# A hybrid decoder layer on one core: matmul order anew around the state scan, two scan products on four quarters, w_out's low parts by VectorE

## The chip, the core and the metric

The kernel runs on one core of one Trainium2 chip. The metric is the device time of one execution in microseconds (us). A figure is the median of several runs; the profile shows one execution.

## What is computed

One decoder layer for 512 positions of width 1024. The reference, cut to what matters here:

```python
h = rms_norm(x, pre_mix_norm)
proj = einsum('bsd,dc->bsc', h, w_in)        # q, k, v | qkv of the delta net | z | a | b
o_att = moba_attention(q, k, v, rel_bias)    # 8 heads of 64, blocks of 256 keys
o_gdn = gated_deltanet(qkv, z, a, b, ...)    # 8 heads of 64, chunks of 64
mix = einsum('bsc,cd->bsd', concatenate([o_att, o_gdn]), w_out)
x = x + rms_norm(mix, post_mix_norm)
h = rms_norm(x, pre_mlp_norm)
m = square(relu(h @ w_up)) @ w_down          # 1024 -> 4096 -> 1024
return x + rms_norm(m, post_mlp_norm)

# the scan in gated_deltanet, chunk by chunk
v_new = u_c - w_c @ state
o = q_c @ state + a_c @ v_new
state = state * gl + k_c^T @ v_new
```

## The kernel before, in words

All large products are made of three matmuls of rounded halves (high by high, low by high, high by low), so every weight chunk of 128x512 is loaded on SP's queue, cast to its high part on ACT (`wo_h`, `w_hi`) and subtracted to its low part (`wo_l`, `w_lo`). `load_split` (L116 to L123) does that for w_out; in the kernel before, its subtraction for w_out is on POOL. The raw chunks rotate through two buffers (`raws`, `w_raw`), so a load waits for the subtraction two chunks earlier.

The stages overlap. A main stream (`projections`) makes the 28 column blocks of h times w_in in the order of the string `ORDER`; it serves as filler. Beside it run `chunks` (normalisation, decay factors and the masked products of the delta net, four times), `inverse` (a triangular inverse by VectorE and small transfers), `scores` and `values` (attention), then `scan`, and after it `weights_out`, `output` and the MLP. PE's order is written out: the class `Weave` (L28 to L67) runs these streams as generators on an estimated PE clock `now`; a stream yields a delay from the table `WAIT` (or the name of a mark) and is resumed no earlier than that; of those that are ready the one of the lowest `RANK` goes first. So a number in `WAIT` moves matmuls on PE. On the other engines a scheduler orders the instructions, with `LEAD` as a priority for some streams. All engines work through their instructions in order.

In `scan` (L735 to L842) a tile t is 128 positions, two chunks c. For each tile: `U V` (tile names `vB,UT`, into the two banks `vo[0]`, `vo[1]`), for each chunk `S,LWQ` (state by the chunk's queries and keys), the copy of `vn` out of the bank (L818), `vn,kdec` (the update of the state), and at the tile's end `A' V` (`vn,AT`, into the other halves of the same banks), whose result ACT copies to `ot` (L839). U V and A' V have 16 products of 64x64 each, two matmul instructions to a product; a 64-row half of the array is chosen by c, a 64-column half by the rows of the bank that are written. `finish_o` (L847 on) normalises `ot` on DVE (L856) and transposes it on PE (`ident,ot`).

In attention, `scores` makes for a group p of two heads four products `pt` of 512, 384, 256 and 128 columns, DVE adds the bias and takes the minimum (L651, reading the bank `ps_a`), ACT takes the exponential (L653), PE transposes it (`ident,L`), ACT copies it (`ph`, L679) and PE multiplies it by V (`ph,V`). There are four groups, 0 to 3. `RC` (L508) is a DVE step of `chunks` whose result PE multiplies by `picks`.

`output` (L900 to L939) makes for each of four position tiles 48 matmuls `wo_h`, `wo_l` by `mg`, `ma`; a tile's two banks are chosen in `start`; `normed` (L940 on) normalises the result (L943, L948, L954) and PE transposes it (`ident,xs`). `up0` starts the MLP.

Of the kernel before, what the change touches and what calls it, by code (L numbers as in the profile page):

```python
# [16 lines left out]
DRAM = bass.MemoryType.DRAM  # L17
EPS = 1e-6

WAIT = {'h': 1.7, 'conv_k': 5.5, 'k': 3.6, 'conv_q': 6.15, 'q': 4.5, 'conv_v': 11.0, 'v': 6.02, 'z': 6.39, 'ab': 0.1, 'g': 11.93, 'scalars': 3.68, 'r_in': 0.8, 'r_out': 4.4, 'kk': 2.46, 'kk_out': 14.43, 'gl': 3.22, 'qk': 3.88, 'va': 1.1, 'a': 2.4, 'row': 1.38, 'rows': 4.0, 'pv': 1.54, 'att': 2.16, 'inverse': 0.9, 'merge': 10, 'p1': 1.5, 'p2': 1.7, 'w': 1.78, 'vn': 1.0, 'state': 1.12, 'o_in': 6.0, 'o': 3.3, 'wo': 0.88, 'wo_out': 17.6, 'normed': 6.44, 'n': 1.7, 'up': 1.9, 'sums': 1.5, 'turned': 0.5, 'pv0': 1.5}  # L20

RANK = {'chunks': 5, 'inverse': 3, 'scan': 3, 'scores': 4, 'values': 2, 'finish_o': 1, 'take': 4}
LEAD = {'chunks': 0, 'inverse': 100, 'scan': 100, 'scores': 0, 'values': 100, 'finish_o': 0, 'take': 0, 'take_a': 0}
START = (5.5, 9.0, 17, 16, 30, 10.5)
ORDER = "q0 k0 x0 k1 q1 q2 k2 k3 z0 q3 y0 x1 v0 w0 v1 y1 w1 v2 x2 v3 x3 y2 w2 y3 z1 w3 z2 z3"


class Weave:  # L28
# [38 lines left out]
def layer(ctx, tc, nc, x, w_in, w_ab, w_out, w_up, w_down, conv_w, a_log, dt_bias, gdn_norm_w, rel_bias,  # L67
# [96 lines left out]
    def kof(pair, k, cols=slice(0, 512)):  # L164
        return pair[k // 4][:, k % 4, cols]
# [259 lines left out]
    def scalars():  # L425

        w8 = lambda t: t[:, :128].rearrange("p (a b) -> p a b", a=8)
        abr = w8(tmp("abr"))
        abw = tmp("abw", FR)[:, :256].rearrange("p (k a b) -> p k a b", k=8, a=2)
        abh, abl = abw[:, :, 0], abw[:, :, 1]  # L430
        nc.sync.dma_start(abr, w_ab)
        yield "h2"
        split(abh, abl, abr)
        abT = bank(shape=(128, 4, 16))
        p_ab = bank()
        yield "h3"
        for k in range(8):
            mm(p_ab[:32], abw[:, k].rearrange("p a b -> p (a b)"), kof(hT_h, k), start=k == 0, stop=False, skip_group_check=True)
            mm(p_ab[:16], abh[:, k], kof(hT_l, k), start=False, stop=k == 7, skip_group_check=True)
        abs_ = tmp("abs")[:32]  # L440
        nc.scalar.copy(abs_, p_ab[:32])
        two = gpool.tile([32, 16], FT, name="two")
        tt(two, ident[:32, :16], ident[:32, 16:32], op=OP.add)
        yield WAIT["ab"]
        for t in range(4):
            mm(abT[:, t, :], abs_[:, 128 * t:128 * t + 128], two, start=True, stop=True)
        ab = gpool.tile([128, 4, 16], FT, name="ab")
        nc.scalar.copy(ab, abT)
# [286 lines left out]
    def scan():  # L735
# [62 lines left out]

        rows_c = [(slice(64 * c, 64 * c + 64), slice(64 - 64 * c, 128 - 64 * c)) for c in range(2)]
        head = lambda h: slice(64 * (h % 2), 64 * (h % 2) + 64)  # L800
        for t in range(4):
            o = sc.tile([128, 512], FT, name="ot", bufs=4)
            V = sc.tile([128, 512], FT, name="vn", bufs=1)
            vo = [bank(shape=(128, 4, 128)) for c in range(2)]
            for h in range(8):
                for c, (cs, _) in enumerate(rows_c):
                    mm(vo[c][cs, h // 2, head(h)], UT[cs, h, t], vB[cs, t, 64 * h:64 * h + 64], start=h == 0, stop=False, skip_group_check=True)
            weave.now -= 8 * 64 * 4 / 2400
            for c, (cs, oc) in enumerate(rows_c):
                n = 2 * t + c  # L810
                S, Sn = SS[n % 2], SS[(n + 1) % 2]
                if n:
                    for p in range(4):
                        wq = LWQ[p // 2][:, p % 2, t, c]
                        mm(vo[c][cs, p], wq[:, :64], S[:, p], start=False, stop=False, skip_group_check=True)
                        mm(vo[c][oc, p], wq[:, 64:], S[:, p], start=p == 0, stop=False, skip_group_check=True)
                    weave.now -= 4 * 128 * 4 / 2400
                nc.scalar.copy(V[cs], vo[c][cs].rearrange("p a b -> p (a b)"))  # L818
                yield WAIT["vn"]
                if n < 7:  # L820
                    sp = bank(shape=(128, 4, 64))
                    for h in range(8):
                        mm(sp[head(h), h // 2], kdec[cs, t, 64 * h:64 * h + 64], V[cs, 64 * h:64 * h + 64], start=True, stop=True)
                    weave.now -= 4 * 64 * 4 / 2400
                    for hh in range(2):
                        hs = head(hh)
                        if n:
                            tt(Sn[hs, :, hs], S[hs, :, hs], EGL[hs, :, n:n + 1].to_broadcast([64, 4, 64]), op=OP.mult)
                            tt(Sn[hs, :, hs], Sn[hs, :, hs], sp[hs], op=OP.add)
                        else:  # L830
                            nc.vector.tensor_copy(Sn[hs, :, hs], sp[hs])
                if c == 0:
                    yield WAIT["state"]
# [41 lines left out]
    def weights_out():  # L875
        yield "scan"
        for b in range(2):
            for z in (1, 0):
                if (b, z) == (1, 0):
                    mark("wo0", 2)  # L880
                    yield "projected"
                wh, wl = big("wo_h", dt=FR), big("wo_l", dt=FR)
                for k in range(4):
                    load_split(wh[:, k], wl[:, k], w_out[512 * z + 128 * k:512 * z + 128 * k + 128, 512 * b:512 * b + 512],
                               sub=nc.gpsimd.tensor_tensor)
                    W[b, 4 * z + k] = (wh[:, k], wl[:, k])
                    yield WAIT["wo"]
        mark("wo", WAIT["wo_out"])

    def output():  # L890
# [550 lines left out]
```

## Time and profile before

| | us |
|---|---|
| median of 3 runs | 662.05 (661.96 to 663.56) |
| profiled execution | 662.51 |
| its span in the trace | 660.7 |
| PE busy in the span | 632.4 |
| DVE busy | 437.6 |
| ACT busy | 360.5 |
| POOL busy | 200.0 |

The span runs from the first to the last instruction that the profiler saw; 1.8 us of the execution's time lie around it. Times in rows are counted from the span's start. Busy is the time in which an engine had an instruction at work; a matmul's listed duration holds its way through the array, so the distance between the starts of two rows says better what the first one took.

### The profile page before, as it was taken

What the parts mean: (1) busy time and instruction counts of PE and PEld (TensorE: products, weight loads), DVE (VectorE), ACT (ScalarE), POOL (GpSimd) and SP (SyncE); (2) the same over time, 40 slices, a digit from 0 to 9 for tenths busy, and PEclk for the clock granted to TensorE, in tenths of its full rate; (3) what the DMA queues carried; (4) which work ended last, traced back from release to release, by engine and by line L of the source; (5) the groups of instructions that cost most, each with busy time, mean ns of one, the idle gap of its engine ahead of it and who ended that gap; (6) DMA issues with size and microseconds to landing.
All of it is one profiled execution on the core that took longest, in us unless ns stands there. A gap on an engine that the chain in (4) does not pass through costs nothing.

```text
span 660.7 us, 11130 instructions
## 1 busy us (share of the span) xinstructions
PE 632.4 (96%) x4357; PEld 526.9 (80%) x4357; DVE 437.6 (66%) x627; ACT 360.5 (55%) x602; POOL 200.0 (30%) x231
## 2 busy tenths in 40 slices
PE   7899999899999999898999999999999999999995
PEld 4778777676687776676799899999998888887884
DVE  4358675997421335365445578878779888988775
ACT  5366564264636646854231675566566556665661
POOL 4355655332454236632302113111130130000002
PEclk9999999999999999999999999999999999999998
DMA  7232323223631202481249989899899999957503
GB/s 235 68 103 71 81 81 103 89 81 112 136 87 51 82 30 84 144 269 65 97 169 332 227 225 238 232 288 284 236 263 328 291 287 291 277 198 288 198 1 127
DMA packets 60226, 113.16 MB, mean 171 GB/s; under 512 B 15700, under 2 KB 34644, under 8 KB 59790
## 3 DMA queue, kind: packets, MB, share of 16 engines
q1 hardware_dynamic: 42446, 83.03, 36.4%
q0 software_dynamic: 17728, 29.43, 21.6%
q8 instruction: 34, 0.56, 0.3%
q14 instruction: 18, 0.15, 0.1%
HBM read 106.65 MB, written 35.15 MB: 215 GB/s over the span
## 4 chain that ended last, share of the span: by engine, by line
PE 80%; DVE 9%; ACT 5%; DMA 3%; POOL 1%; issue 1%; SPq 0%; DVEq 0%; POOLq 0%; ACTq 0%
PE ps_mm L77 41%; PE ps_g L77 21%; PE ps_a L77 14%; PE ps_a L81 2%; DVE conv L346 2%; PE ps_g L81 1%; DMA w_raw<-in_w_out 1%; DVE inv L726 1%; DVE pr L725 1%; DMA xx<-in_x 1%; DMA wd<-d_T 1%; DMA inv<-d_n 1%; ACT wo_h L122 1%; ACT ph L679 0%; DVE xs L948 0%
## 5 line engine op out<-in xcount | busy, mean ns | idle before, releaser
L135 POOL TENSOR_TENSOR w_lo<-w_raw,w_hi 128x512 fp32r<-128x512 f32 x54 | 70.7, 1311 | 116.1 <-ACT w_hi L134 115.8
L77 PE MATMUL ps_mm<-hT_h,w_hi 128*128 128x512 f32 (+1 forms) x224 | 93.1, 416 | 1.0 <-DVE conv L346 1.0
L77 PE MATMUL ps_mm<-hT_l,w_hi 128*128 128x512 f32 (+1 forms) x224 | 87.2, 389 | 0.0
L77 PE MATMUL ps_mm<-hT_h,w_lo 128*128 128x512 f32 (+1 forms) x224 | 86.7, 387 | 0.0
L110 ACT CAST wdh<-wd 128x1024 fp32r<-128x1024 f32 x53 | 55.9, 1054 | 52.0 <-PE ps_mm L77 23.5
L111 DVE TENSOR_TENSOR u_l<-w,u_h 128x1024 fp32r<-128x1024 f32 x46 | 56.2, 1224 | 37.8 <-ACT u_h L110 36.8
L111 DVE TENSOR_TENSOR wdl<-wd,wdh 128x1024 fp32r<-128x1024 f32 x53 | 64.9, 1225 | 22.8 <-ACT wdh L110 22.7
L110 ACT CAST u_h<-w 128x1024 fp32r<-128x1024 f32 x46 | 47.9, 1045 | 57.1 <-PE ps_a L77 19.7
L1123 POOL DMA_DIRECT2D d_T<-in_w_down x32 | 33.0, 1034 | 144.1 <-DMA d_T<-in_w_down 80.5
L134 ACT CAST w_hi<-w_raw 128x512 fp32r<-128x512 f32 x56 | 34.6, 620 | 46.0 <-PE ps_mm L77 26.2
L77 PEld LDWEIGHTS ps_mm<-hT_h,w_hi 128*128 128x128 f32 x224 | 42.8, 191 | 14.5 <-issue 6.3
L77 PEld LDWEIGHTS ps_mm<-hT_h,w_lo 128*128 128x128 f32 x224 | 43.0, 192 | 9.0
L77 PEld LDWEIGHTS ps_mm<-hT_l,w_hi 128*128 128x128 f32 x224 | 43.0, 192 | 6.4 <-DVE hT_l L111 0.2
L77 PE MATMUL ps_mm<-wdh,u_h 128*128 128x512 f32 x116 | 45.3, 390 | 0.0
L168 POOL TENSOR_SCALAR s<-s 128x1 f32<-128x1 f32 x12 | 3.8, 319 | 136.8 <-DVE s L1316 108.2
L77 PE MATMUL ps_mm<-wdl,u_h 128*128 128x512 f32 x116 | 45.1, 389 | 0.0
L77 PE MATMUL ps_mm<-wdh,u_l 128*128 128x512 f32 x116 | 45.1, 389 | 0.0
L346 DVE SCALAR_TENSOR_TENSOR conv<-ps_mm,cw,conv 128x511 f32<-128x511 f32 (+2 forms) x36 | 26.8, 745 | 18.0 <-ACT conv L343 17.5
L111 DVE TENSOR_TENSOR u_l<-f,u_h 128x1024 fp32r<-128x1024 f32 x28 | 34.1, 1219 | 0.0
L77 PE MATMUL ps_g<-wdh,u_h 128*128 128x512 f32 x80 | 31.2, 390 | 0.4 <-DVE y L1297 0.4
L651 DVE CUSTOM_DVE_ANT_0 L<-ps_a,E 128x512 f32<-128x512 f32 (+3 forms) x32 | 14.4, 487 | 25.7 <-PE ps_a L77 25.5
L77 PE MATMUL ps_g<-wdh,u_l 128*128 128x512 f32 x80 | 31.1, 389 | 0.0
(428 smaller groups left out, 1751.7 us busy)
## 6 DMA issues: line engine op xcount, KB each, us to landing
d_T<-in_w_down POOLq DMA_DIRECT2D x48, 512.0 KB, 10.6
wd<-d_T SPq DMA_DIRECT2D x32, 512.0 KB, 6.2
w<-in_w_up SPq DMA_DIRECT2D x28, 512.0 KB, 8.5
w_raw<-in_w_in SPq DMA_DIRECT2D x54, 256.0 KB, 2.6
wd<-in_w_down SPq DMA_DIRECT2D x24, 512.0 KB, 7.7
w_raw<-in_w_out SPq DMA_DIRECT2D x16, 256.0 KB, 2.7
d_T<-d_T POOLq DMA_DIRECT2D x8, 512.0 KB, 10.5
xx<-in_x SPq DMA_DIRECT2D x4, 512.0 KB, 6.6
```

What stands on the lines that cost most here:

```text
L77: nc.tensor.matmul(o, l, r, **kw)
L81: nc.tensor.transpose(o, i, ident[:k, :k])
L110: nc.scalar.copy(hi, src)
L111: tt(lo, src, f32(hi), op=OP.subtract)
L122: nc.scalar.copy(hi, raw)
L134: nc.scalar.copy(hi, raw)
L135: (sub or tt)(lo, raw, f32(hi), op=OP.subtract)
L346: stt(c[:, s:], p[:, :512 - s], cw[:, ft, j:j + 1], c[:, s:], op0=OP.mult, op1=OP.add)
L651: nc.vector.tensor_tensor_reduce(out=l, in0=s[hh][:, :w], in1=Es[hh][:, w - 1::-1], scale=1.0, scalar=3e38, op0=OP.add, op1=OP.min, accum_ ...
L725: tt(v, iN[:, 0:m, m:m + 1].to_broadcast([128, m, w]), iU[:, m:m + 1, m:32].to_broadcast([128, m, w]), op=OP.mult)
L726: tt(iU[:, 0:m, m:32], iU[:, 0:m, m:32], v, op=OP.subtract)
L1123: nc.gpsimd.dma_start(d_T[t][k], block(b, second)[k], accum_op=OP.add, max_dma_last_dim=1024)
```

## The change

- The tables. `WAIT`: k 3.6 to 2.95, z 6.39 to 7.99, r_in 0.8 to 0.72, gl 3.22 to 2.12, va 1.1 to 1.38, rows 4.0 to 3.2, att 2.16 to 1.3, o_in 6.0 to 3.6, o 3.3 to 3.73, normed 6.44 to 11.21. The others as in the diff.
- U V of the next tile and A' V of this tile are written in turn, so that consecutive matmuls go to four 64x64 quarters of the array. U V of both chunks is now in one bank `vb[t]`, A' V of both in one bank `ob[t]`.
- a, b: the matmuls of the low half take the 32 columns that those of the high half take (before 16).
- w_out's low parts are subtracted by VectorE.
- The output's position tiles take other banks.

```diff
-RANK = {'chunks': 5, 'inverse': 3, 'scan': 3, 'scores': 4, 'values': 2, 'finish_o': 1, 'take': 4}
-LEAD = {'chunks': 0, 'inverse': 100, 'scan': 100, 'scores': 0, 'values': 100, 'finish_o': 0, 'take': 0, 'take_a': 0}
-START = (5.5, 9.0, 17, 16, 30, 10.5)
-ORDER = "q0 k0 x0 k1 q1 q2 k2 k3 z0 q3 y0 x1 v0 w0 v1 y1 w1 v2 x2 v3 x3 y2 w2 y3 z1 w3 z2 z3"
+RANK = {'chunks': 5, 'inverse': 3, 'scan': 3, 'scores': 5, 'values': 5, 'finish_o': 1, 'take': 4}
+LEAD = {'chunks': 0, 'inverse': 0, 'scan': 100, 'scores': 0, 'values': 100, 'finish_o': 0, 'take': 0, 'take_a': 100}
+START = (5.5, 9.0, 17, 16, 30, 9.0)
+ORDER = "q0 k0 x0 k1 q1 q2 k2 k3 z0 q3 y0 x1 v0 w0 v1 y1 w1 v2 v3 x2 y2 w2 x3 y3 z1 w3 z2 z3"
...
-            mm(p_ab[:16], abh[:, k], kof(hT_l, k), start=False, stop=k == 7, skip_group_check=True)
+            mm(p_ab[:32], abw[:, k].rearrange("p a b -> p (a b)"), kof(hT_l, k), start=False, stop=k == 7, skip_group_check=True)
...
+        vb, ob = [bank(shape=(128, 4, 128))], []
+        def apart(t, V=None):
+            for h in range(8):
+                for c, (cs, oc) in enumerate(rows_c):
+                    if t < 4:
+                        mm(vb[t][cs, h // 2, head(h)], UT[cs, h, t], vB[cs, t, 64 * h:64 * h + 64], start=h == 0, stop=False, skip_group_check=True)
+                if V is not None:
+                    for c, (cs, oc) in enumerate(rows_c):
+                        mm(ob[t - 1][oc, h // 2, head(h)], AT[cs, h, t - 1], V[cs, 64 * h:64 * h + 64], start=t == 1 and not c and h == 0, stop=True, skip_group_check=True)
...
+        apart(0)
         for t in range(4):
...
-            vo = [bank(shape=(128, 4, 128)) for c in range(2)]
-            for h in range(8):
-                for c, (cs, _) in enumerate(rows_c):
-                    mm(vo[c][cs, h // 2, head(h)], UT[cs, h, t], vB[cs, t, 64 * h:64 * h + 64], start=h == 0, stop=False, skip_group_check=True)
+            ob.append(bank(shape=(128, 4, 128)))
...
-            for h in range(8):
-                for c, (cs, oc) in enumerate(rows_c):
-                    mm(vo[c][oc, h // 2, head(h)], AT[cs, h, t], V[cs, 64 * h:64 * h + 64], start=not t and not c and h == 0, stop=True, skip_group_check=True)
+            if t < 3:
+                vb.append(bank(shape=(128, 4, 128)))
+            apart(t + 1, V)
...
-                    load_split(wh[:, k], wl[:, k], w_out[512 * z + 128 * k:512 * z + 128 * k + 128, 512 * b:512 * b + 512],
-                               sub=nc.gpsimd.tensor_tensor)
+                    load_split(wh[:, k], wl[:, k], w_out[512 * z + 128 * k:512 * z + 128 * k + 128, 512 * b:512 * b + 512])
...
-            part[t] = [bank(("mm", "g")[t % 2]) for b in range(2)], xs
+            part[t] = [bank(i) for i in (("mm", "mm"), ("g", "g"), ("g", "mm"), ("mm", "g"))[t]], xs
```

Three places in the order of instructions. First, PE at the end of the scan's tile 0 and the start of tile 1 (`vn,kdec` updates the state, `vn,AT` is A' V, `vB,UT` is U V, `hT` by `w` is the projection, `ph,V` attention). Before:

```order
L77 MATMUL ps_g<-vn,kdec 64x64 x8
L77 MATMUL ps_g<-vn,AT 64x64 x16
L77 MATMUL ps_mm<-hT_h_82,w_hi 128x512
L77 MATMUL ps_mm<-hT_l_84,w_hi 128x512
L77 MATMUL ps_mm<-hT_h_82,w_lo 128x512
L77 MATMUL ps_a<-ph,V 64x256 x2
```

Six projection matmuls and `ph,V` lay between A' V and U V of tile 1. Now U V of tile 1 is in turn with A' V of tile 0, eight times two and two:

```order
L77 MATMUL ps_g<-vn,kdec 64x64 x8
L77 MATMUL ps_g<-vB,UT 64x64 x2
L77 MATMUL ps_g<-vn,AT 64x64 x2
L77 MATMUL ps_g<-vB,UT 64x64 x2
L77 MATMUL ps_g<-vn,AT 64x64 x2
```

Second, DVE around the `RC` step of `chunks` that PE waits for (`conv` is the causal convolution, L560 to L568 the masked products). Before, three convolution steps and five others stood ahead of it:

```order
L572 TENSOR_TENSOR kbe<-rkb,egc 128x32
L346 SCALAR_TENSOR_TENSOR conv<-ps_mm,cw,conv 128x511
L346 SCALAR_TENSOR_TENSOR conv<-ps_mm,cw,conv 128x510
L346 SCALAR_TENSOR_TENSOR conv<-ps_mm,cw,conv 128x509
L560 TENSOR_TENSOR NT<-ps_g,AT 128x256
L560 TENSOR_TENSOR NT<-ps_a,AT 128x256
L568 TENSOR_TENSOR LWQ_97<-LWQ_97,ps_g 128x8x64
L567 TENSOR_TENSOR AT<-ps_g,AT 128x256
L567 TENSOR_TENSOR AT<-ps_a,AT 128x256
L350 SCALAR_TENSOR_TENSOR LWQ_97<-th,conv 128x8x64
L508 SCALAR_TENSOR_TENSOR RC_120<-RH,su,RT 32x512
```

Now it stands ahead of them:

```order
L572 TENSOR_TENSOR kbe<-rkb,egc 128x32
L508 SCALAR_TENSOR_TENSOR RC_120<-RH,su,RT 32x512
L541 CAST RG<-RC_120 32x8
L346 SCALAR_TENSOR_TENSOR conv<-ps_mm,cw,conv 128x511
L560 TENSOR_TENSOR NT<-ps_g,AT 128x256
```

Third, the last group of scores (group 3) and the loads of w_out. Before, PE made that group's `pt` between tiles 2 and 3 of the scan. The first product of the scan (`uap,NT`) comes 24 projection matmuls earlier now. DVE at that group before, with nothing of w_out on it:

```order
L852 TENSOR_REDUCE oss<-osq 128x8
L651 ISA L,mins<-ps_a,E 128x384
L651 ISA mins 128x1
L651 ISA L,mins<-ps_a,E 128x384
L651 ISA mins 128x1
L829 TENSOR_TENSOR S_2441<-S_2441,ps_g 64x4x64 x2
L651 ISA L,mins<-ps_a,E 128x256
```

Now the group comes after the scan, with w_out's subtractions and a step of z (`zs`, which waits for ACT) in DVE's row ahead of its blocks:

```order
L867 TENSOR_TENSOR ot<-ot,oss 128x512
L651 ISA L,mins<-ps_a,E 128x384
L651 ISA mins 128x1
L123 TENSOR_TENSOR wo_l<-w_raw,wo_h 128x512
L415 SCALAR_TENSOR_TENSOR zs<-t_2992,zs 128x512
L123 TENSOR_TENSOR wo_l<-w_raw,wo_h 128x512
L651 ISA L,mins<-ps_a,E 128x256
```

and on PE the group's end stands with three projection matmuls left to lay between:

```order
L81 MATMUL ps_a<-ident,L 128x128 x4
L77 MATMUL ps_mm<-hT_h_82,w_hi 128x512
L77 MATMUL ps_mm<-hT_l_84,w_hi 128x512
L77 MATMUL ps_mm<-hT_h_82,w_lo 128x512
L77 MATMUL ps_a<-ph,V 64x128 x2
L81 MATMUL ps_a<-ident,L 128x128 x6
L77 MATMUL ps_a<-ph,V 64x256 x2
L77 MATMUL ps_a<-ph,V 64x384 x2
L81 MATMUL ps_a<-ident,L 128x128 x8
L81 MATMUL ps_g<-ident,ot 128x128 x16
L81 MATMUL ps_a<-ident,R_3089 128x128 x4
```

On SP's queue the sixteen loads of w_out stood as eight, two loads for the MLP (`E`), six and two more; now six, the two `E` (whose buffers the last group of scores sets free), and ten more with two `t2` loads among them. In `output`, both position tiles 0 and 1 are transposed (`ident,xs`) after all 48 matmuls of tile 2, tile 3's transposes come last, directly ahead of the second half of `up0`.

## Rows read from the trace of the kernel before

**Rows 1.** The page's first section: busy time and share of each engine.
```profile
PE 632.4 (96%) x4357; PEld 526.9 (80%) x4357; DVE 437.6 (66%) x627; ACT 360.5 (55%) x602; POOL 200.0 (30%) x231
```

**Rows 2.** Windows: length, then busy time by engine, granted clock, DMA share, GB/s.
```profile
120.00:140.00 20.00, 17.27 (x87) 12.35 (x86) 19.55 (x47) 8.81 (x23) 6.00 (x5) 1.00 0.19 66
...
400.00:500.00 100.00, 100.00 (x833) 99.82 (x833) 80.97 (x81) 62.76 (x82) 21.57 (x28) 1.00 0.98 253
```

**Rows 3.** Waits of PE from 40 to 346 us: total us, times, longest.
```profile
PE ps_a L81 <- DVE xs L954: 1.9, 2, 1.2
PE ps_a L77 <- DVE mins L651: 1.7, 1, 1.7
PE ps_a L81 <- ACT ph L679: 1.3, 4, 0.6
PE ps_mm L77 <- DVE xs L948: 1.3, 1, 1.3
PE ps_g L77 <- ACT vn L818: 1.3, 1, 1.3
PE ps_g L77 <- DVE RC L508: 1.2, 1, 1.2
PE ps_g L81 <- DVE ot L856: 1.1, 1, 1.1
...
PE ps_mm L77 <- DVE conv L346: 1.0, 1, 1.0
PE ps_g L77 <- ACT LWQ L788: 0.6, 1, 0.6
```

**Rows 4.** Timeline of DVE from 95 us: start, duration, instruction, idle before.
```profile
95.32 2.32 DVE L346 SCALAR_TENSOR_TENSOR conv<-ps_mm,cw,conv 128x511 f32<-128x511 f32 x3 [1.51 <-ACT conv L343]
...
100.19 0.75 DVE L508 SCALAR_TENSOR_TENSOR RC<-RH,su,RT 32x512 fp32r<-32x512 f32 x1
```

**Rows 5.** Timeline of PE in the scan.
```profile
196.66 2.21 PE L77 MATMUL ps_g<-uap,NT 32*32 32x32 f32 x128
...
207.30 0.69 PE L77 MATMUL ps_g<-UT,kB 64*64 64x64 f32 x32
...
240.68 0.51 PE L77 MATMUL ps_g<-vn,kdec 64*64 64x64 f32 x10
...
242.22 0.50 PE L77 MATMUL ps_mm<-hT_h,w_hi 128*128 128x512 f32 x1
...
243.82 1.15 PE L77 MATMUL ps_g<-vB,UT 64*64 64x64 f32 x32
244.90 1.09 PE L77 MATMUL ps_g<-S,LWQ 128*64 128x128 f32 x16
```

**Rows 6.** Windows of 1 us around the wait for vn, columns as in rows 2.
```profile
259.00:260.00 1.00, 0.13 (x1) 0.00 (x0) 0.32 (x2) 1.00 (x4) 0.76 (x1) 1.00 0.60 215
...
261.00:262.00 1.00, 1.00 (x7) 0.71 (x3) 0.84 (x2) 1.00 (x4) 1.00 (x1) 0.59 0.38 131
262.00:263.00 1.00, 1.00 (x6) 0.54 (x6) 0.00 (x0) 0.51 (x2) 1.00 (x2) 0.50 0.35 131
...
264.00:265.00 1.00, 1.00 (x7) 0.50 (x7) 1.00 (x3) 0.97 (x3) 1.00 (x1) 0.70 0.11 27
```

**Rows 7.** Groups by form, 245 to 346 us: busy, mean ns of one, idle before.
```profile
L123 POOL TENSOR_TENSOR wo_l<-w_raw,wo_h 128x512 fp32r<-128x512 f32 x16 | 21.2, 1327 | 18.9 <-ACT wo_h L122 18.8
...
L111 DVE TENSOR_TENSOR ma_l<-ps_a,ma_h 128x512 fp32r<-128x512 f32 x4 | 2.8, 690 | 3.4 <-ACT ma_h L110 3.4
...
L414 ACT ACTIVATE t<-zs 128x512 f32<-128x512 f32 x2 | 1.3, 630 | 0.1
...
L679 ACT COPY ph<-ps_a 128x384 f32<-128x384 f32 x2 | 0.9, 477 | 0.0
```

**Rows 8.** One tile's instructions and transfers, w_raw, 240 to 290 us.
```profile
L121 SPq DMA_DIRECT2D w_raw<-in_w_out x16: 327/328/787, 246.0 to 284.7; - x16
...
DMA to landing us min/median/max: 2.5/2.7/8.0
```

More of the change, by code (lines that the diff above doesn't have):

```diff
@@ L18 @@
 EPS = 1e-6
-WAIT = {'h': 1.7, 'conv_k': 5.5, 'k': 3.6, 'conv_q': 6.15, 'q': 4.5, 'conv_v': 11.0, 'v': 6.02, 'z': 6.39, 'ab': 0.1, 'g': 11.93, 'scalars': 3.68, 'r_in': 0.8, 'r_out': 4.4, 'kk': 2.46, 'kk_out': 14.43, 'gl': 3.22, 'qk': 3.88, 'va': 1.1, 'a': 2.4, 'row': 1.38, 'rows': 4.0, 'pv': 1.54, 'att': 2.16, 'inverse': 0.9, 'merge': 10, 'p1': 1.5, 'p2': 1.7, 'w': 1.78, 'vn': 1.0, 'state': 1.12, 'o_in': 6.0, 'o': 3.3, 'wo': 0.88, 'wo_out': 17.6, 'normed': 6.44, 'n': 1.7, 'up': 1.9, 'sums': 1.5, 'turned': 0.5, 'pv0': 1.5}
-RANK = {'chunks': 5, 'inverse': 3, 'scan': 3, 'scores': 4, 'values': 2, 'finish_o': 1, 'take': 4}
-LEAD = {'chunks': 0, 'inverse': 100, 'scan': 100, 'scores': 0, 'values': 100, 'finish_o': 0, 'take': 0, 'take_a': 0}
-START = (5.5, 9.0, 17, 16, 30, 10.5)
-ORDER = "q0 k0 x0 k1 q1 q2 k2 k3 z0 q3 y0 x1 v0 w0 v1 y1 w1 v2 x2 v3 x3 y2 w2 y3 z1 w3 z2 z3"
+WAIT = {'h': 1.7, 'conv_k': 5.5, 'k': 2.95, 'conv_q': 6.15, 'q': 4.5, 'conv_v': 11.0, 'v': 6.02, 'z': 7.99, 'ab': 0.1, 'g': 11.93, 'scalars': 3.68, 'r_in': 0.72, 'r_out': 4.4, 'kk': 2.46, 'kk_out': 14.43, 'gl': 2.12, 'qk': 3.88, 'va': 1.38, 'a': 2.4, 'row': 1.38, 'rows': 3.2, 'pv': 1.54, 'att': 1.3, 'inverse': 0.9, 'merge': 10, 'p1': 1.5, 'p2': 1.7, 'w': 1.78, 'vn': 1.0, 'state': 1.12, 'o_in': 3.6, 'o': 3.73, 'wo': 0.88, 'wo_out': 17.6, 'normed': 11.21, 'n': 1.7, 'up': 1.9, 'sums': 1.5, 'turned': 0.5, 'pv0': 1.5}
+RANK = {'chunks': 5, 'inverse': 3, 'scan': 3, 'scores': 5, 'values': 5, 'finish_o': 1, 'take': 4}
+LEAD = {'chunks': 0, 'inverse': 0, 'scan': 100, 'scores': 0, 'values': 100, 'finish_o': 0, 'take': 0, 'take_a': 100}
+START = (5.5, 9.0, 17, 16, 30, 9.0)
+ORDER = "q0 k0 x0 k1 q1 q2 k2 k3 z0 q3 y0 x1 v0 w0 v1 y1 w1 v2 v3 x2 y2 w2 x3 y3 z1 w3 z2 z3"
 class Weave:
@@ L800, in scan @@
         head = lambda h: slice(64 * (h % 2), 64 * (h % 2) + 64)
+        vb, ob = [bank(shape=(128, 4, 128))], []
[7 more added lines that the diff above has]
+                        mm(ob[t - 1][oc, h // 2, head(h)], AT[cs, h, t - 1], V[cs, 64 * h:64 * h + 64], start=t == 1 and not c and h == 0, stop=True, skip_group_check=True)
+            n = 8 * ((t < 4) + (V is not None))
+            weave.now -= n * 64 * 4 / 2400 * (1.5 if n == 16 else 1)
+        apart(0)
         for t in range(4):
@@ L803, in scan @@
             V = sc.tile([128, 512], FT, name="vn", bufs=1)
-            vo = [bank(shape=(128, 4, 128)) for c in range(2)]
-            for h in range(8):
-                for c, (cs, _) in enumerate(rows_c):
-                    mm(vo[c][cs, h // 2, head(h)], UT[cs, h, t], vB[cs, t, 64 * h:64 * h + 64], start=h == 0, stop=False, skip_group_check=True)
-            weave.now -= 8 * 64 * 4 / 2400
+            ob.append(bank(shape=(128, 4, 128)))
             for c, (cs, oc) in enumerate(rows_c):
@@ L814, in scan @@
                         wq = LWQ[p // 2][:, p % 2, t, c]
-                        mm(vo[c][cs, p], wq[:, :64], S[:, p], start=False, stop=False, skip_group_check=True)
-                        mm(vo[c][oc, p], wq[:, 64:], S[:, p], start=p == 0, stop=False, skip_group_check=True)
+                        mm(vb[t][cs, p], wq[:, :64], S[:, p], start=False, stop=False, skip_group_check=True)
+                        mm(ob[t][oc, p], wq[:, 64:], S[:, p], start=p == 0, stop=False, skip_group_check=True)
                     weave.now -= 4 * 128 * 4 / 2400
-                nc.scalar.copy(V[cs], vo[c][cs].rearrange("p a b -> p (a b)"))
+                nc.scalar.copy(V[cs], vb[t][cs].rearrange("p a b -> p (a b)"))
                 yield WAIT["vn"]
@@ L833, in scan @@
                     yield WAIT["state"]
-            for h in range(8):
-                for c, (cs, oc) in enumerate(rows_c):
-                    mm(vo[c][oc, h // 2, head(h)], AT[cs, h, t], V[cs, 64 * h:64 * h + 64], start=not t and not c and h == 0, stop=True, skip_group_check=True)
-            weave.now -= 8 * 64 * 4 / 2400
+            if t < 3:
+                vb.append(bank(shape=(128, 4, 128)))
+            apart(t + 1, V)
             for c, (cs, oc) in enumerate(rows_c):
-                nc.scalar.copy(o[cs], vo[c][oc].rearrange("p a b -> p (a b)"))
+                nc.scalar.copy(o[cs], ob[t][oc].rearrange("p a b -> p (a b)"))
             yield WAIT["state"]
```

## The prediction

> **What bounds the kernel now.** The page's first section says it at once: PE is at work for 632.4 of the span's 660.7 us, the next engine for 437.6 [rows 1]. The windows say where that is not so. From 400 to 500 us, in the MLP, PE is busy for 100.00 of 100.00 us [rows 2], and the change touches nothing there, so a gain can only come from the mixing stages before about 346 us: from PE's waits, from matmuls that take longer than they need, and from a lower granted clock. The list of PE's waits between 40 and 346 us has all three handles [rows 3]: nine kinds of wait together make 11.4 us, and each names the instruction that ended it. The timelines then say what that instruction stood behind.
>
> **Part 1, waits that go in the first half.** RC's wait of 1.2 us [rows 3] ends at a DVE step which starts at 100.19, after three convolution steps of 2.32 us together [rows 4]. RC now stands ahead of them, so I take the 1.2 as gone. The next two waits, 1.0 for the convolution and 1.7 for the scores' minimum [rows 3], lie in a stretch where DVE is busy for 19.55 of 20 us [rows 2]: there DVE sets the time and PE only arrives earlier. DVE's inverse also starts earlier, by about the same 1.2, so the two waits stay about as long; from POOL's steps, between which no subtraction of 1.3 us [rows 7] stands any longer, I add 0.6, half of one. Bounds of this addition: −1.2 (DVE doesn't get ahead and PE waits for it all the same) and 1.3. Sum of part 1: 1.8 us.
>
> **Part 2, the scan.** Tile 0's U V needs one bank instead of two, and the wait of 0.6 for a bank that ACT still reads [rows 3] goes. U V alone takes 1.08 us by the distance of the starts at 243.82 and 244.90, on two quarters of the array; A' V has the same shape. Thirty-two matmuls of the same 64x64 on four quarters took 0.69 us [rows 5]. So the 64 of U V and A' V in turn should take about 2 × 0.65 = 1.3 us in place of 2 × 1.08, a saving of 0.86, three times: 2.6 us. The ends: nothing, if the quarters don't overlap, and 3 × 1.08 = 3.2, if the second product is wholly hidden. I take 2.6, since the row with four quarters is the nearest.
>
> The rule that speaks against this stands in the Trainium skill, TensorEngine Tiling (Array Packing), Restrictions and Gotchas: row tiles cannot use one PSUM bank at the same time, and the change puts both row halves of U V into one bank. By that rule U V and A' V, each in its bank, would go one half after the other. The trace bears on it: `uap,NT` has two row halves and one bank at a time, and its 128 matmuls of half the width take 2.21 us [rows 5], 17 ns each. U V's take 1.15 us for 32 on two quarters, 72 ns in each quarter, so half the width is 36 ns, and two at a time 18. One at a time would have been 4.6 us. The trace speaks against the rule here.
>
> The wait of 1.3 us for `vn` [rows 3] arises where ACT casts w_out's chunks between the scan's copies; now only the casts of w_in are there. With it goes what came of it: PE stood for most of the microsecond at 259, and at 261 the granted clock fell to the lower of its levels (1.2 GHz), 0.59, 0.50, 0.50 (the row left out is like the one ahead) and 0.70 of full speed in four windows [rows 6]. That is 0.41 + 0.5 + 0.5 + 0.3 = 1.7 us of lost speed. Sum of part 2: 0.6 + 2.6 + 1.3 + 1.7 = 6.2 us.
>
> **Part 3, the output.** Waits of 1.3 (L948, tile 2's bank still being read) and 1.9 (L954, transposes that come before the normalised tile) [rows 3] go: tile 2 now takes its first bank from those that are free, and all transposes stand behind tile 2's 48 matmuls. 3.2 us. In exchange tile 3's transposes stand directly ahead of matmuls that need them cast and subtracted: a cast and a subtraction of 128x512, 0.6 and 0.69 us [rows 7], of which the second bank's overlap the first's. Estimate 0.9, between 0.5 and 1.3.
>
> **Part 4, the end of attention.** Here the waits of 1.3 (`ph`, four times) and 1.1 (`ot`) [rows 3] go as they were, 2.4 us, and new ones come. Group 3's scores now stand after the scan, with few projection matmuls between, and ACT and DVE have w_out's casts and subtractions ahead of their steps. What PE then waits for, by estimate:
> - `pt128` needs a bank that DVE frees only after two subtractions and the z step, 3 × 0.69, and two passes of 0.35, while PE has 1.4 of its own: 1.35.
> - `ph,V` 384 waits for ACT's z steps and two copies, 0.6 + 0.63 + 2 × 0.48 = 2.2 [rows 7], with at most 0.6 of PE work beside: 1.6, and up to 0.4 where a w_out cast stands between: 2.0.
> - The first block behind a subtraction 0.1, `ph` of the last block 0.7, `ot` 0.4.
>
> Sum 4.5 us. The ends: 0, if the queues have room that I don't see, and 7, if the casts wait for transfers of 2.7 us [rows 8]; another 1.7 if one of these waits lowers the clock as at 259.
>
> **Free edits.** a, b by 32 columns: the eight matmuls stream the same positions, so nothing. w_out's subtraction moves 16 × 1.33 = 21 us off POOL [rows 7], on to DVE at 16 × 0.69 = 11; DVE is not the bound at 280 us, and what it delays is counted in part 4. A shorter subtraction also frees the raw buffers sooner.
>
> **Sum.** 1.8 + 6.2 + 3.2 + 2.4 = 13.6 less 0.9 + 4.5 = 5.4 makes 8.2 us. The profiled execution took 662.51 and would take 654.3; the median of the runs is 0.5 lower, so I forecast **654.0 us**. Its own range, with the bounds of the terms not all at one end, is 651 to 657.
>
> **The rivals.**
> - **New waits are hidden.** If ACT and DVE keep up after the scan, the 4.5 falls to 1 or less: 650. For it speaks that a shorter subtraction makes w_out's stream lighter, against it the order of the rows. 0.12.
> - **The end of attention eats more.** 7 us there and one fall of the clock, 1.7, in place of 4.5: 658. For it speaks that eight handovers between four engines have almost no filler left. 0.13.
> - **The banks take turns.** By the mechanism of part 2, U V and A' V together take 2.16, as before, and U V of tile 0 and A' V of tile 3, alone, 2.16 in place of 1.08: the 2.6 turns into −2.2, and the time is 658.8. The trace speaks against it; 0.04.
> - **w_out starves the output, slower than before.** Ten loads stand behind the two `E`, which wait for the last minimum of the scores. By the starts of 246.0 and 284.7 a load came every 38.7 / 15 = 2.58 us [rows 8]. The output begins about 10 us after that minimum and needs the last chunk some 20 us later (84 matmuls at no more than 0.27). Two `t2` loads of the same size stand among the ten. Twelve at 2.58 take 31 us, and the cost is 1; at 3.4 (2.7 to land and a cast of about 0.6, with nothing beside them) they take 41, and the output starves for 11: 654 + 11 = 665. The point is 3.2 us a load, where 12 × 3.2 = 38 eats the 8.2. Against it: two raw buffers let a load run beside the last one's subtraction. 0.10.
> - **The moves don't matter.** If DVE's chain holds part 1 and new waits match the old ones, the time is within 2 us of 662. 0.06.
>
> My forecast's own case has the remaining 0.55.
>
> **The numbers.** A measurement of this kernel can tell 0.3% (2.0 us) from no change. Faster by more: the forecast, the first three rivals less a little of the second, 0.82. Same: 0.08. Slower: 0.10. The range from 648.5 to 660.5 takes in the forecast, the first and third rival and most of the second: 0.82.
>
> **What would show it.** U V and A' V together in about 1.3 us, three times; no wait at RC, `vn`, L948 or L954; the granted clock at 1.00 from 40 to 346 us; the first product of the scan near 190 us, not 196.66; the first `wo_h` matmul some 7 us earlier; new waits of PE for L651 and `ph` around 250 to 275; a gap of 0.9 ahead of `up0`'s second half; POOL less busy by 21 us, DVE more by 11. The prediction is wrong if U V and A' V take 2.2 us, if PE waits for `wo_h` or `wo_l` by more than 2 us, or if the waits around the last scores add up to more than 7.

## The result and the profile after

The changed kernel takes 657.7 us (656.89 to 658.4, 4 runs) beside 662.54 of the kernel before: a ratio of 0.9932 with a 95% interval of 0.9915 to 0.9949. By the ratio that is 4.5 us less than before (the medians differ by 4.8), not the 8.2 of the sum. Measured once more beside later experiments it took 659.64 beside 662.88, ratio 0.9945 (0.9926 to 0.9964). The profiled execution has a span of 656.1 us, 4.6 less than before.

The page's first section answers to [rows 1]:

```profile
PE 630.3 (96%) x4357; PEld 523.6 (80%) x4357; DVE 445.9 (68%) x643; ACT 358.9 (55%) x602; POOL 180.5 (28%) x215
```

POOL lost 19.5 us and DVE gained 8.3, near the 21 and 11 of the prediction. The list of PE's waits from 40 to 346 us answers to [rows 3]; columns as there:

```profile
PE ps_mm L77 <- ACT wo_h L122: 1.7, 1, 1.7
PE ps_a L77 <- DVE mins L651: 1.7, 1, 1.7
PE ps_g L81 <- DVE kbe L572: 1.5, 1, 1.5
PE ps_g L81 <- DVE om L876: 1.1, 1, 1.1
PE ps_g L81 <- ACT th L348: 1.1, 1, 1.1
PE ps_g L81 <- DVE R L499: 1.1, 1, 1.1
PE ps_mm L77 <- DVE conv L346: 1.0, 1, 1.0
PE ps_a L81 <- DVE ma_l L111: 0.6, 1, 0.6
PE ps_mm L77 <- DVE ma_l L111: 0.3, 1, 0.3
PE ps_a L81 <- ACT ph L679: 0.2, 1, 0.2
PE ps_mm L77 <- ACT ma_h L110: 0.2, 1, 0.2
PE ps_mm L77 <- DVE wo_l L123: 0.2, 1, 0.2
```

The waits for `xs`, `vn`, `RC` and `LWQ` are gone, as forecast. But three stand there that the prediction did not have: `wo_h` (1.7), `kbe` (1.5) and a longer one for `R` (1.1). The wait for `R` stood in the list of before too, with

```profile
PE ps_g L81 <- DVE R L499: 0.4, 1, 0.4
```

Three milestones say in which stretch the time went: the scan's first product and the first `wo_h` matmul now, and that `wo_h` matmul before (last row).

```profile
192.40 2.21 PE L77 MATMUL ps_g<-uap,NT 32*32 32x32 f32 x128
275.69 0.48 PE L77 MATMUL ps_mm<-wo_h,mg_h 128*128 128x512 f32 x1
282.02 0.50 PE L77 MATMUL ps_mm<-wo_h,mg_h 128*128 128x512 f32 x1
```

The scan's first product starts at 192.40 in place of 196.66 [rows 5], 4.3 us earlier. But 24 projection matmuls of 0.23 us, 5.5, that stood ahead of it now come later, so the first part is 1.2 us slower. From the scan's first product to the first `wo_h` matmul it took 85.4 us and now takes 83.3. That way now also holds those 5.5 us, while a `ph,V` of 1.0 has moved behind it, so for the same work it is 6.5 us shorter. Behind the first `wo_h` matmul 0.7 us was lost again.

| stretch | forecast us | measured us |
|---|---|---|
| up to the scan (part 1) | −1.8 | +1.2 |
| scan and end of attention (parts 2 and 4) | −4.1 | −6.5 |
| output (part 3) | −2.3 | +0.7 |
| sum | −8.2 | −4.6 |

The scan's timeline on PE: first U V of tile 0 alone, with the row after it; then the last update of tile 0's state, the first row of U V and A' V behind it, and the projection that follows.

```profile
213.41 1.11 PE L77 MATMUL ps_g<-vB,UT 64*64 64x64 f32 x32
214.46 0.66 PE L81 MATMUL ps_a<-ident,L 128*128 128x128 f32 x4
...
220.51 0.51 PE L77 MATMUL ps_g<-vn,kdec 64*64 64x64 f32 x10
220.80 0.27 PE L77 MATMUL ps_g<-vB,UT 64*64 64x64 f32 x1
...
222.06 0.50 PE L77 MATMUL ps_mm<-hT_h,w_hi 128*128 128x512 f32 x1
```

From 220.51 to 222.06 it takes 1.55 us, of which the pair of U V and A' V has 1.26, from 220.80 on, as its forecast of 1.3. Before, update and A' V alone took 1.54 (240.68 to 242.22), and U V 1.08 more [rows 5]: U V has become free, 1.07 us for each of three tiles, the upper bound of part 2. U V alone, now with both row halves in one bank, takes 1.05: the bank is no hindrance.

The first half, on PE, and then on DVE with one row of POOL:

```profile
85.79 0.63 PE L81 MATMUL ps_g<-ident,R 128*128 128x128 f32 x4 [1.07 <-DVE R L499]
95.27 0.63 PE L81 MATMUL ps_g<-ident,R 128*128 128x128 f32 x4 [1.50 <-DVE kbe L572]
134.17 0.79 PE L77 MATMUL ps_a<-pt 64*128 64x384 f32 x5 [1.69 <-DVE mins L651]
```

```profile
92.96 1.28 POOL L135 TENSOR_TENSOR w_lo<-w_raw,w_hi 128x512 fp32r<-128x512 f32 x1
93.03 1.24 DVE L539 TENSOR_TENSOR rkb<-rkq,beta 128x8 f32<-128x8 f32 x1 [0.85 <-POOL rkq L172]
...
97.25 0.75 DVE L508 SCALAR_TENSOR_TENSOR RC<-RH,su,RT 32x512 fp32r<-32x512 f32 x1 [2.03 <-ACT RT L507]
```

RC comes at 97.25, not at 100.19 [rows 4], and PE doesn't wait for it. But the transposes of R, three projection matmuls earlier, come before DVE has R ready. PE waits 2.57 us there, where it waited 1.2 for RC and 0.4 for R. Most of the second of the two waits is one small step: `rkb`, from which `kbe` is made, took 1.24 us while POOL subtracted `w_lo`. In the kernel before it took 0.17, with no subtraction beside it:

```profile
93.28 0.17 DVE L539 TENSOR_TENSOR rkb<-rkq,beta 128x8 f32<-128x8 f32 x1 [0.37 <-POOL rkq L172]
```

That is 1.07 of the 1.50. Then the wait of 1.69 for the scores' minimum stands as before, and this time the clock falls behind it (windows of 1 us, columns as in [rows 2]):

```profile
133.00:134.00 1.00, 0.00 (x0) 0.00 (x0) 0.97 (x3) 0.00 (x0) 0.00 (x0) 1.00 0.00 0
...
135.00:136.00 1.00, 1.00 (x4) 0.81 (x5) 1.00 (x5) 1.00 (x3) 0.45 (x1) 0.79 0.09 25
136.00:137.00 1.00, 1.00 (x3) 0.77 (x3) 1.00 (x1) 0.76 (x3) 0.83 (x1) 0.50 0.00 0
137.00:138.00 1.00, 1.00 (x4) 0.66 (x2) 1.00 (x6) 0.38 (x1) 0.00 (x0) 0.50 0.13 25
138.00:139.00 1.00, 1.00 (x6) 0.53 (x6) 1.00 (x5) 0.93 (x4) 0.00 (x0) 0.51 0.64 238
```

0.21 + 0.50 + 0.50 + 0.49 = 1.7 us of lost speed: the fall at 261 us [rows 6] is gone, and one of the same price came here. At the output, PE's wait and what SP issued before it:

```profile
292.93 0.49 PE L77 MATMUL ps_mm<-wo_h,ma_h 128*128 128x512 f32 x1 [1.72 <-ACT wo_h L122]
```

```profile
282.94 0.33 SPq L121 DMA_DIRECT2D w_raw<-in_w_out  x1
283.32 0.42 SPq L904 DMA_DIRECT2D nb<-in_post_mix  x1
283.80 0.42 SPq L905 DMA_DIRECT2D nb<-in_pre_mlp  x1
285.60 0.33 SPq L121 DMA_DIRECT2D w_raw<-in_w_out  x1
285.98 1.79 SPq L911 DMA_DIRECT2D xs<-in_x  x2
290.45 0.33 SPq L121 DMA_DIRECT2D w_raw<-in_w_out  x1
```

The load issued at 285.60 was cast at 292.26, after 6.6 us, where the median from issue to landing was 2.7 [rows 8], with four transfers of 512 KB around it. The kernel before had such a load too, of 8.0 [rows 8], but PE did not wait there: its output began 6 us later. The last load, at 290.45, had to wait for the buffer of the load two before.

### The profile page after: what moved, and what is told of

The parts are those of the page before. It is cut to its first block, busy times and chain, and to the rows that moved or that the text cites. A ratio compares the mean times of both kernels' runs of the same rounds, so it can differ in the third digit from the quotient of the medians.

```text
span 656.1 us, 11128 instructions
## 1 busy us (share of the span) xinstructions
PE 630.3 (96%) x4357; PEld 523.6 (80%) x4357; DVE 445.9 (68%) x643; ACT 358.9 (55%) x602; POOL 180.5 (28%) x215
## 4 chain that ended last, share of the span: by engine, by line
PE 82%; DVE 8%; DMA 6%; ACT 2%; issue 1%; POOL 1%; SPq 0%; DVEq 0%; POOLq 0%; ACTq 0%
PE ps_mm L77 43%; PE ps_g L77 22%; PE ps_a L77 14%; DMA w_raw<-in_w_out 3%; PE ps_a L81 2%; PE ps_g L81 1%; DVE inv L726 1%; DVE conv L346 1%; DVE pr L725 1%; DMA xx<-in_x 1%; DMA xy<-d_x 1%; DMA wd<-d_T 1%; DMA inv<-d_n 1%; DVE wo_l L123 1%; POOL rkq L172 0%
## 5 line engine op out<-in xcount | busy, mean ns | idle before, releaser
L77 PE MATMUL ps_g<-wdl,u_h 128*128 128x512 f32 x80 | 31.1, 389 | 0.0
```

## The experiments

All are timed against the kernel before, in executions beside it; waits are from the profile of one execution. "A fall of the clock" is a stretch in which PE's granted clock goes down to 0.50, as at 135 us above. A span is compared with the change's 656.1 and 655.9 where the clock falls at the same places; otherwise the text says what the falls cost. Before 600 us the change's trace has one, of 1.7 us of lost speed, and so has the one of the kernel before.

**1. `k` back.** The number that sets the early transposes.

```diff
-'k': 2.95
+'k': 3.6
```

> The change with one number of the table put back, k from 2.95 to 3.6, which puts the transposes of R of the third and fourth group of chunks three projection matmuls later and RC behind the convolution on VectorE again. Theory A (part 1 failed because those transposes came too early): PE's waits for R (1.07) and kbe (1.50) fall to about 0.4 and 0, the wait for RC of about 1.25 comes back, net 0.9 us less; if the granted clock then stays up at 135 us as in the kernel before, another 1.5 less: 655.3 to 656.8. Rival B (VectorE's inverse sets the time of that stretch, whatever stands ahead of it): the wait for the minimum at about 133 us takes up what was saved, 657.2 to 658.2.

658.81 us, ratio 0.9956 (0.9940 to 0.9971). In the first half theory A held: R 0.4, `kbe` gone, RC 1.2 again, against 2.57 before, while the wait for the minimum grew by 0.2: 0.7 us less. But the sum got no better. A new wait of 1.55 came 150 us later:

```profile
239.44 1.77 DVE L867 TENSOR_TENSOR ot<-ot,oss 128x512 f32<-128x512 f32 x1 [2.60 <-POOL oss L866]
241.24 0.87 DVE L841 TENSOR_TENSOR S<-S,ps_g 64x256 f32<-64x256 f32 x2
```

The scheduler of DVE now puts the product of `ot` ahead of the state's update, and it waits for POOL and then runs at 1.77 us (0.69 in the change) while POOL subtracts `w_lo`. The scan's chain stands behind it. So one number moved PE at 85 us and DVE's order at 240. The profile also has a second fall of the clock, at 295, and is the slowest of this kernel's six executions (661.00; the others 657.34 to 659.65). The waits for `R` and `kbe` come of `k`, but the total doesn't follow from them.

**2. U V and A' V as blocks.** The matmuls of `apart`, same place and banks, in two loops over h.

```diff
             for h in range(8):
                 for c, (cs, oc) in enumerate(rows_c):
                     if t < 4:
...
+            for h in range(8):
                 if V is not None:
```

> The change with U V of the next tile written as one block ahead of A' V, instead of in turn with it; same banks, same place. Theory A (U V is hidden because consecutive matmuls go to four quarters): the block of vn,kdec, U V and A' V takes 2.5 us instead of 1.55, three times, 657.7 + 2.9 = 660.6. Rival B (the saving comes of the place alone, of fewer changes between shapes, or the four quarters are kept busy by matmuls that are further apart in the order): less than 0.5 us slower.

661.53 us, ratio 0.9992 (0.9976 to 1.0007): by the median nothing is left of the gain. The span is 658.1, 2.0 us more than the change's.

```profile
220.46 0.51 PE L77 MATMUL ps_g<-vn,kdec 64*64 64x64 f32 x10
...
222.76 0.50 PE L77 MATMUL ps_mm<-hT_h,w_hi 128*128 128x512 f32 x1
```

The block takes 2.30 us in place of 1.55, three times 0.75: 2.25, where 2.9 was expected, since the ends of the blocks overlap. It is the writing in turn that makes U V free. The median lost more than the span (3.8 us), and the granted clocks go with that: five of the twelve executions had a mean of 0.994, as the profiled one and the change's (0.993 to 0.996), and took 659.30 to 660.28; the other seven had 0.988 to 0.991 and took 661.46 to 663.89. By estimate one fall of 1.7 us in 656 makes 0.0026 of that mean. So at the change's clock the blocks cost some 2.2 us, as in the trace, and the new order keeps a part of the gain without the pairing: the span of 658.1 is 2.6 under the one of the kernel before, with one fall in each.

**3. w_out's subtraction on GpSimd.**

```diff
-w_out[512 * z + 128 * k:512 * z + 128 * k + 128, 512 * b:512 * b + 512])
+w_out[512 * z + 128 * k:512 * z + 128 * k + 128, 512 * b:512 * b + 512], sub=nc.gpsimd.tensor_tensor)
```

> The change with w_out's subtractions on GpSimd again. Theory A (the shorter subtraction frees the raw buffers sooner, and the last chunks of w_out are already late): each load's round is 0.6 us longer, PE waits for the last chunks by 2 to 5 us more than the 1.95 of the change, 659 to 662. Rival B (VectorE's subtractions in the queue ahead of the scores are what costs, the transfers set the loads' pace): the wait for om or ot of 1.1 goes and the wait for w_out stays, 656 to 657.5.

666.86 us, ratio 1.0080 (1.0067 to 1.0093): slower than before. Theory A, and more than its 2 to 5 us:

```profile
298.77 0.79 PE L77 MATMUL ps_mm<-wo_h,ma_h 128*128 128x512 f32 x1 [5.72 <-ACT wo_h L122]
```

The wait for `wo_h` is 5.7 in place of 1.7, a second one for the minimum adds 2.0, and the clock falls twice more, which makes 5.1 of the 8.6 us that the span is longer. This is the rival of the slower side: the new order brings the output some 6 us earlier, and only the shorter subtraction lets w_out follow nearly.

**4. `nb` and `x` loaded later,** behind fifteen of the sixteen loads of w_out.

```diff
         for t in range(2):
             yield from first(t, 1)
+        nc.sync.dma_start(nb[:, 0], post_mix.partition_broadcast(128))
+        for t in range(2):
+            nc.sync.dma_start(part[t][1][:, 1], x[128 * t:128 * t + 128, :])
+        nc.sync.dma_start(nb[:, 1], pre_mlp.partition_broadcast(128))
```

> The change with the loads of nb (two, 512 KB each) and of the first two x tiles issued after the output's second half of w_out has begun, behind fifteen of the sixteen w_out loads, instead of among the last three. Theory A (those transfers slowed the last w_out chunks from 2.7 to over 6 us): the waits of 1.72 and 0.23 for w_out go, 655.8. Rival B (the last load is late because its raw buffer is freed late, or the output then waits for nb): 657.2 to 658.5.

659.78 us, ratio 0.9965 (0.9952 to 0.9978), no faster, and slower than either theory had it. The two chunks that were late came in time, but the last one fell behind the moved transfers:

```profile
288.57 0.62 ACT L122 CAST wo_h<-w_raw 128x512 fp32r<-128x512 f32 x1
289.39 0.62 ACT L122 CAST wo_h<-w_raw 128x512 fp32r<-128x512 f32 x1 [0.20 <-DMA w_raw<-in_w_out]
299.92 0.62 ACT L122 CAST wo_h<-w_raw 128x512 fp32r<-128x512 f32 x1 [7.81 <-DMA w_raw<-in_w_out]
```

It was issued at 290.42, took 9.5 us, and PE waited 2.5; behind that wait, at 300, the clock fell a second time, for 1.7 of the 2.8 us that the span is longer. So both halves hold: the other transfers slow the chunks, and two raw buffers hold the last load back.

**5. The scan's part alone** in the kernel before: `apart` and its banks, nothing else.

```diff
-            vo = [bank(shape=(128, 4, 128)) for c in range(2)]
+            ob.append(bank(shape=(128, 4, 128)))
...
+            if t < 3:
+                vb.append(bank(shape=(128, 4, 128)))
+            apart(t + 1, V)
```

> The kernel before with the scan's part of the change alone (U V of the next tile in turn with A' V of this one, one bank each), all tables, w_out's subtractions on GpSimd and the output's banks as before. Theory A (the quarters save 0.75 to 1.07 us a tile, and the bank's wait of 0.6 goes, whatever stands around): 662.1 less 2.9 to 3.8, 658.3 to 659.2. Rival B (the chain of the state sets that stretch in the old order, as the wait for vn shows; what PE saves, it then waits): 660.5 to 662.5.

664.44 us, ratio 1.0043 (1.0021 to 1.0064), slower: a miss for theory A, and above the range of rival B.

```profile
260.54 0.68 PE L77 MATMUL ps_g<-vn,kdec 64*64 64x64 f32 x16 [2.26 <-ACT vn L830]
```

Before, that product started at 260.40 after a wait of 1.3 [rows 3]; now PE is there earlier and waits 2.26 to the same time. In the old order ACT sets the time of `vn`: ahead of the copy at 259.91 it had two casts of w_out, the first after 1.20 us without its load, and four steps of the scores. PE's saving turns into waiting. A second fall of the clock, 1.7 of the 1.8 us that the span is longer, and waits of 0.8 and 0.7 for the first `mg` followed. Beside experiment 2 this says: by the medians neither half gains alone, the order without the pairing 0.9992, the pairing without the order 1.0043, both 0.9932; by the spans the order gains 2.6 and the pairing in the old order nothing.

**6. The output's old banks.**

```diff
-            part[t] = [bank(i) for i in (("mm", "mm"), ("g", "g"), ("g", "mm"), ("mm", "g"))[t]], xs
+            part[t] = [bank(("mm", "g")[t % 2]) for b in range(2)], xs
```

> The change with the output's banks as before, mm and g in turn by position tile. Theory A (the wait for L948 of 1.3 went by the banks, that for L954 of 1.9 by the later transposes): the wait of 1.3 comes back, 1.3 us slower than the change. Rival B (the later order alone took both away): no difference over 0.5 us.

660.79 us, ratio 0.9973 (0.9957 to 0.9989). The span is 657.2, 1.1 more than the change's, and the wait for the first step of `normed` (L948 before, L958 here) is back with 1.4: theory A.

**7. Four raw buffers for w_out:** every second load goes to `kB` or `vn`, which the scan has left, by one more argument of its `load_split`.

```diff
+raw=sc.tile([128, 512], FT, name=("kB", "vn")[k // 2], bufs=1) if k % 2 else None
```

> The change with four raw buffers for w_out instead of two (the free kB and vn of the scan as third and fourth), so that a load no longer waits for the subtraction two chunks earlier, and nb comes behind nearly all w_out loads. Theory A (the late last chunks of w_out, a matter of two raw buffers and of nb's transfers in front, cost PE 1.95 us): these waits go and nothing takes their place, 1.5 to 2.0 us faster than the change, 655.7 to 656.2 by its median. Rival B (casts and subtractions that come earlier hold up the scores' steps on ScalarE and VectorE instead): the waits for ph, the minimum or om grow by as much, 657 to 659.

658.40 us, ratio 0.9951 (0.9934 to 0.9968); the span is 655.0, 1.1 less than the change's. The waits for `wo_h` and `wo_l` are gone, that for `om` fell to 0.8, and two came for `ph`, 0.53 and 1.01 together:

```profile
271.46 1.24 PE L77 MATMUL ps_a<-ph,V 128*64 128x384 f32 x4 [1.01 <-ACT ph L679]
```

The waits are as theory A has them, what took their place as rival B: casts that come earlier hold up attention's copies on ACT. The median doesn't tell it from the change.

**8. Four buffers, `k` back, `ot` on GpSimd** for tiles 0 to 2.

```diff
-        tt(e8(o), e8(o), r[:, :, None].to_broadcast([128, 8, 64]), op=OP.mult)
+        (nc.gpsimd.tensor_tensor if t < 3 else tt)(e8(o), e8(o), r[:, :, None].to_broadcast([128, 8, 64]), op=OP.mult)
```

> Four raw buffers as in the run before, k put back to 3.6, and the product of ot with its norm for the first three tiles by GpSimd, so that it cannot stand ahead of the state's update on VectorE, which had cost the run with k alone a wait of 1.55 us. Theory A (each wait is what it seems): the first half gains 0.7, the wait of 1.55 does not come, and w_out's 1.95 goes: 2.5 us or more faster than the change, below 655.3. Rival B (the wait for the minimum at 133 us or the granted clock takes up what the first half saves): as with four buffers alone.

657.69 us, ratio 0.9943 (0.9921 to 0.9966). No wait for the state's update came, none for `wo_h`, no fall at 135 us; but the wait for `om` rose to 2.8, `ph` is 1.6, and in the profiled execution, the slowest of six, the clock fell behind them. No better than the change; each wait removed showed the next.

This trace says something of the clock too. PE waits 1.69 us ahead of the matmuls of a, b in the change and here, in the same place of the order; here the clock fell behind it, there it did not. The matmul that waited and a window behind it, first here, then in the change:

```profile
23.28 0.39 PE L77 MATMUL ps_g<-hT_h,abw 128*32 128x512 f32 x1 [1.69 <-DVE two L443]
24.00:25.00 1.00, 1.00 (x4) 0.48 (x3) 0.00 (x0) 0.00 (x0) 0.00 (x0) 0.50 0.07 16
24.32 0.39 PE L77 MATMUL ps_g<-hT_h,abw 128*32 128x512 f32 x1 [1.69 <-DVE two L443]
25.00:26.00 1.00, 1.00 (x6) 0.50 (x5) 0.00 (x0) 0.00 (x0) 0.00 (x0) 1.00 0.06 16
```

And the wait of 1.9 for the minimum at about 134 is the same here and in experiment 1; there the clock fell behind it, here it did not.

**9. The change again,** with no edit.

> The change itself once more, beside the runs of this call, so that these are compared on one chip. Both theories: 0.993 of the time of the kernel before, 657.5 to 658.5.

659.64 us, ratio 0.9945, span 655.9, with the same waits (2.0 for `wo_h`) and the same fall at 135 us. The median misses the expected 657.5 to 658.5. Five of the six executions had a mean granted clock of 0.991 to 0.993; the profiled one, with 0.996, took 657.67.

**10. A fill at the first scores:** nine projection matmuls more between the first group's products of 512 and 384 columns.

```diff
-                yield WAIT["row"]
+                yield WAIT["row"] + (2.0 if (p, q) == (0, 3) else 0)
```

> The change with one delay more: the first group's scores of 384 columns come 2.0 us of PE's estimated clock later, so that nine projection matmuls more stand between them and those of 512. Theory A (the wait of 1.69 for the minimum at 133 us and the fall of the granted clock behind it are PE's to fill): both go, 1.7 and 1.5 us, and the fillers are not missed later: 3 us faster than the change, 654.5. Rival B (VectorE's inverse is late by as much and the next wait is for it, or the fillers are missing at the end of attention): less than 1 us faster.

657.65 us, ratio 0.9941 (0.9912 to 0.9971); span 655.1. The wait of 1.69 went and a longer one took its place at the next product, for the same engine:

```profile
140.43 0.62 PE L77 MATMUL ps_a<-pt 64*128 64x256 f32 x5 [2.65 <-DVE mins L651]
```

DVE, full with the inverse, sets the time here, as rival B has it. The clock did not fall anywhere between 40 and 600 us in this trace, though this wait is longer than the one it fell behind in the change. That saves 1.7, the longer wait takes 0.9 of it, and the span is shorter by 0.8 to 1.0. The medians of experiments 9 and 10 differ by 2 us, their intervals overlap; two of the seven executions here, with 0.986 and 0.989, took 662.3 and 662.4.

**11. Fill and four buffers,** the edits of experiments 7 and 10 together.

> The same fill and four raw buffers for w_out together. Theory A (the two add up): 3 us and 1.1 us, 653.5. Rival B (with fewer fillers left, the waits for ph and om that four buffers brought grow): no faster than the fill alone.

659.54 us, ratio 0.9949 (0.9929 to 0.9969), span 656.6 without a fall before 600 us: rival B, `om` 1.6 and `ph` 1.7.

No version is surely faster than the change.

## Why the prediction was right, and where its size was wrong

The direction and the range held (657.7 in 648.5 to 660.5), and so did the main reason: waits and lost speed between the scan and the output, not work. The forecast of 654.0 is 3.7 us too low, and in part its errors cancel: by the table, parts 1 and 3 came out 6.0 us worse than forecast, parts 2 and 4 together 2.4 better. That the second made up for some of the first was luck: without it the time would have stood at the upper end of the range. Of its own signs, the waits at RC, `vn`, L948 and L954 went; the granted clock did not stay at 1.00; and the wait for w_out, 1.95 us here and 2.2 in experiment 9, stands at the 2 us that it had named as a sign of being wrong. By its own steps:

- **Part 1 failed.** "I take the 1.2 as gone" was right of RC, and the term left out what the same move makes late: the step ahead of RC. PE's transposes of R were put three matmuls earlier, and the waits for `R` and `kbe`, 1.07 + 1.50, outweigh the 1.2. Experiment 1 shows that the number `k` does it, by two ways: the earlier place, and `rkb` falling beside a subtraction of POOL, 1.07 of the 1.50 (with `k` back it takes 0.17 again). The list that the prediction added up has eleven kinds of wait, not nine, and the 0.4 for `R` is one of the two left out. The code of the change sets those transposes by `k`; the sum did not count them. Of the inverse "starts earlier", the opposite is true: its first step on DVE is at 116.5 us, 1.1 later.
- **The clock** was counted as won (1.7). The fall at 261 went, one of the same price came at 135, behind a wait that stood before with 1.70 and cost no clock there. That is the other half of the miss up to the scan, in part made up before 192. The fall came at 134 to 136 in eight of the eleven traces in the new order, in none of the two in the old.
- **Part 2** was undersized: 3.2 for the quarters, the upper end, in place of 2.6. The waits for the bank and for `vn` went as forecast. The rival of the banks fell by the row at 213.41: 1.05 us for U V in one bank, where taking turns would have made 2.16. The Trainium skill (TensorEngine Tiling (Array Packing), Restrictions and Gotchas) says that different row tiles cannot access one PSUM bank at the same time. For U V, whose two row halves write different partitions of the bank, the traces do not agree: 1.05 us in one bank, 1.08 in two.
- **Part 3 failed by w_out.** 3.2 us of waits went, the banks holding 1.1 to 1.4 of it (experiment 6). In their place came 1.7 + 0.2 for the last chunk but one of w_out and 0.6 for a bank at the transposes, and at `up0` 0.5 in place of 0.9. The prediction had this mechanism as its rival of the slower side and priced it all or nothing, from 3.2 us a load; it set in for the last three loads, cast 5.0 to 6.6 us after their issue, one of which PE waited for. What slowed them, the transfers of `nb` and `x` (experiment 4), the rival left out.
- **Part 4** was oversized: of 4.5 us came the 1.1 for `om` and some 0.7 inside `ph,V` (eight matmul instructions of 256 and 384 positions took 2.0 us, before 1.23). The waits for the `pt` products and most of those for the copies did not come: ACT and DVE kept up.
- **Free edits**: the eight matmuls of a, b took 397 ns each, before 391, and PE's wait of 1.7 ahead of them stands in both traces. Nothing, as taken. That w_out's subtraction is free was true only in one direction: undone, it costs 9 us (experiment 3), over half of it by the clock.

What the total would be without the fall of the clock was not isolated: where it falls changes with the experiment and, behind the same wait, with the execution (experiment 8). Which waits bring it about stays open.

## What to carry to other kernels

When a step is moved earlier, look for the input of that step, not only for the step that used to wait. A saving on the busiest engine counts only where no other engine sets the time of its next wait: the same pairing gained 2 to 4 us in one order and lost 0.4% in another, where a longer wait and a fall of the clock took it. One profiled execution shows one draw of the clock: before two versions are compared by their medians, look at the granted clock of each execution. And a term "wait removed" needs the next wait's name and its distance, since most of the runs here that removed the wait they aimed at found another close behind it.

## What was not expected of the hardware

- Products of 64x64 that alternate between the array's diagonal and its other two quarters cost nothing beside each other: 1.55 us with U V, 1.54 without. The same matmuls as two blocks cost 0.75 more; only the blocks' ends overlapped.
- PE's clock fell behind a wait of 1.69 us at 133, but not behind one of 1.70 at the same place before, nor behind one of 2.65 at 138 in experiment 10. Behind the wait of 1.69 ahead of a, b it fell in the profiled execution of experiment 8 and not in that of the change. A fall cost 1.7 us wherever it was summed but once (3.4 in experiment 3, behind the wait of 5.7), as much as the wait of 1.7 itself.
- Four transfers of 512 KB beside a load of 256 KB stretched it from a median of 2.7 to 6.6 us, and to 9.5 in experiment 4.
- A VectorE step of 128x8 took 1.24 us beside a subtraction of 128x512 on GpSimd, and 0.17 without one; one of 128x512 took 1.77 beside it, and 0.69 without (experiment 1).
